# A fused decoder layer on one core: turning the gate's head pairs one at a time in buffers of their own, and issuing one kind of write from ScalarE

## The chip, the cores and the metric

The kernel runs on one core of one Trainium2 chip. The metric is device time of one execution in microseconds (us), the median of several runs. A kernel has five instruction streams: TensorE (PE, matrix products and 128x128 transposes), VectorE (DVE), ScalarE (ACT), GpSimd (POOL) and SyncE (SP). Each stream runs in order: an instruction that waits holds everything behind it on its own engine. DMA transfers are issued by SP, POOL or ACT, and run beside the engines.

## The reference

One decoder layer on 256 tokens of width 2048, all in float32: a normalised input goes through one wide projection, then through two token mixers, whose outputs are gated, projected, merged and added back.

```
h = rms_norm(x, pre_norm_w);  proj = h @ w_in
# A, gated delta rule, 8 heads x 128: conv + silu on q, k, v; chunks of 64 tokens
T = inverse(I + L);  u = T @ vb;  w = T @ kb;  scan over the chunks;  norm;  * silu(gdn_z)
# B, block attention, 8 heads x 128: at 256 tokens one block, so plain causal attention
p = softmax(mask(q @ k.T * scale));  ob = (p @ v) * silu(moba_z)
merged = sigmoid(gate_a) * (oa @ w_branch_a) + sigmoid(gate_b) * (ob @ w_branch_b)
out = x + rms_norm(merged @ w_out, post_norm_w)
```

The change concerns B: the factor `silu(moba_z)`, called `zm` here ("the gate"), and the probabilities `p`.

## The kernel before, in words

Every projection multiplies in three parts: a float32 weight block is cast by ScalarE into `hi` (line 256) and VectorE subtracts to get `lo` (line 257); PE then runs `hi` and `lo` products (line 167 is the helper that records every matmul). The weights arrive by DMA from SP into three rotating buffers, and the `hi`/`lo` pairs rotate over three more, so a cast can begin when PE has finished the block three before it. A block of a head projection is 16 matmuls. PE runs these projections back to back, block after block, in the order of the list `ORDER` (line 47): `zm0 zm1` are the gate's two projections, `mv0 mv1` attention's values, `v3` the last pair of values of mixer A, and `mk0 ... mk3` the query and key projections (`mq`, `mk`) of the four head pairs of mixer B.

Everything else is put between the projections by queues of generators. Each generator runs some instructions and yields a number, the wait until its next step, counted in half units per small group of matmuls (`tick`, line 159). Several queues advance beside each other; within one queue, one generator follows the other. `pin` (line 164) keeps an instruction in program order with the other pinned ones of its engine; what isn't pinned may be moved by the program's scheduler.

Four pieces of work of this kind meet around the change:

- **Inverse** (`inverse`, line 705): VectorE works out T in 63 steps on the tile `tv` (lines 726 and 733). Then POOL writes it to DRAM (`t_d`, line 737) and loads it back in another layout (`inv`, line 750). PE transposes it (`tl`) soon after.
- **Values of A** (`v_tok`, line 786): VectorE transposes in 32x32 blocks, and `moved` (line 779) finishes the transposition by a write to DRAM (line 783) and a load back (line 784): here `vx`.
- **Gate** (`turned_gate`, line 1250): the gate has tokens on the partitions and must have channels there. For each head pair VectorE makes two block transposes (line 1257) into the scratch `spare`, which is the last quarter of the tile `ga_`, and `moved` brings them back over `zm`. One generator does all four pairs, one after the other, in the queue `bq`; it starts with `mk0`. The scratch is one for all four pairs, and the same one that the probabilities use.
- **Attention** (`attend`, line 1190): scores `ms` on PE, softmax on VectorE and ScalarE, block transposes of the probabilities into `spare` (line 1222), `moved` with the write `pT_d` and the load `pT`, and after a wait of 5 the products `po` (lines 1232 and 1233), which read `pT`. VectorE multiplies them with the turned gate (line 1234).

In `moved`, both the write and the load are issued by POOL and pinned, so POOL's order is the order of the program: whoever comes later waits until the earlier transfers may be issued. The load must wait on POOL until the write has landed.

Of the kernel before, what the change touches and what calls it, by code (L numbers as in the profile page):

```python
# [15 lines left out]
P = 128  # L16
# [23 lines left out]
A_WAIT2 = 1.5  # L40
A_WAIT3 = 5
A_WAIT4 = 1
G_WAIT = 1.5

# [48 lines left out]
def hybrid_layer(  # L95
# [15 lines left out]
    nc = tc.nc  # L111
    B, S, D = x.shape
    NT = S // P
    KT = D // P
    H = a_log.shape[1]
# [31 lines left out]
    def aux_tile(name):  # L147
        return aux.tile([P, 512], F32, tag="aux", name=name)

    gq, vq, mq = Queue(), Queue(), Queue()  # L150
    aq, bq = Queue(), Queue()
# [3 lines left out]
    extra = []  # L155
# [8 lines left out]
    pin = tc.keep_in_program_order  # L164

    def mm(*args, **kwargs):
        return pin(nc.tensor.matmul(*args, **kwargs))  # L167
# [496 lines left out]
    zg, zm = z_tiles["zg"], z_tiles["zm"]  # L664
# [14 lines left out]
    def silu_gate(n, c):  # L679
        c0, c1 = (ZG[c], ZG[c + 1]) if n == "zg" else (c * 512, (c + 1) * 512)  # L680
        silu_out(n, c0, c1, proj_n(w_in, {"zg": CZ, "zm": CMZ}[n] + c0, hT, KT, f"{n}{c}", c1 - c0))
# [3 lines left out]
    def keys(p):  # L685
        pk = proj_t(CK + 2 * p * P, f"k{2 * p}")
        kTs[p] += [halves(pk[m], f"k{2 * p + m}") for m in range(2)]
        for m in range(2):
            conv_silu(kTs[p][m], H + 2 * p + m)

    def queries(p):
        h = 2 * p
        pq = proj_t(CQ + h * P, f"q{h}")
        qTs = [halves(pq[m], f"q{h + m}") for m in range(2)]
        for m in range(2):
            conv_silu(qTs[m], h + m)
        gq.add(score_pair(h, kTs[p], qTs))
        if p == H // 2 - 1:
            gq.add(inverse())
            gq.add(solve())  # L700
# [75 lines left out]
            nc.vector.tensor_scalar_mul(inv[t][lo_, :, 64:128], pb[t][lo_], -1.0)  # L776
        yield SV_WAIT

    def moved(blocks, back, name):

        n = blocks.shape[1] // 4
        d = dram.tile([4, P, n], F32, name=f"{name}_d")
        pin(nc.gpsimd.dma_start(d.rearrange("i (r j) x -> (i r) (j x)", j=4), blocks))
        pin(nc.gpsimd.dma_start(back.rearrange("p (i x) -> p i x", i=4), d.rearrange("i k x -> k i x")))

    def v_tok(h, vTs):
# [23 lines left out]
    def values(p):  # L810
        h = 2 * p
        pv_ = proj_t(CV + h * P, f"v{h}")
        vTs = [halves(pv_[m], f"v{h + m}") for m in range(2)]
        for m in range(2):
            conv_silu(vTs[m], 2 * H + h + m)
        vq.add(v_tok(h, vTs))
        v_left[0] -= 1
        after[0] = SLOW

    ga_ = big.tile([P, D // 512, NT, 512], F32, tag="ga", name="ga")  # L820

    spare = ga_[:, D // 512 - 1].rearrange("p t n -> p (t n)")
# [19 lines left out]
    def sigmoid_gate(n, col, c):  # L842
        pts = proj_n(w_in, col + c * 512, hT, KT, f"{n}{c}")
        for t in range(NT):
            nc.scalar.activation(gate_place(n, c, t), pts[t], AF.Sigmoid, scale=rstd[:, t : t + 1])
# [336 lines left out]
    def attention_values(c):  # L1182
        pts = proj_n(w_in, CMV + c * 512, hT, KT, f"mv{c}")
        for t in range(NT):
            nc.scalar.activation(mv[:, t, c * 512 : (c + 1) * 512], pts[t], AF.Copy, scale=rstd[:, t : t + 1])
# [4 lines left out]
    def attend(h, qTs, kTs):  # L1190
        yield A_WAIT1
        ss, mxs, sms = [], [], []
        for m in range(2):
            qT, kT = qTs[m], kTs[m]
            ps = aux_tile(f"ms_{h + m}")
            mm(ps[:, 0:P], qT[:, :P], kT[:, :P], start=True, stop=True)
            mm(ps[:, P : 3 * P], qT[:, P:], kT, start=True, stop=True)
            s = wk.tile([P, 3 * P], F32, tag="s", name=f"s_{h + m}")
            mx = wk.tile([P, 2], F32, tag="mx", name=f"mx_{h + m}")
            sm = wk.tile([P, 2], F32, tag="sm", name=f"sm_{h + m}")  # L1200
            nc.vector.scalar_tensor_tensor(
                s[:, 0:P], ps[:, 0:P], qscale[:, 0:1], mask_m[:, P:], op0=ALU.mult, op1=ALU.add
            )
            nc.vector.scalar_tensor_tensor(
                s[:, P:], ps[:, P : 3 * P], qscale[:, 1:2], mask_m, op0=ALU.mult, op1=ALU.add
            )
            nc.vector.tensor_reduce(mx[:, 0:1], s[:, 0:P], axis=AX.X, op=ALU.max, negate=True)
            nc.vector.tensor_reduce(mx[:, 1:2], s[:, P:], axis=AX.X, op=ALU.max, negate=True)
            nc.scalar.activation(s[:, 0:P], s[:, 0:P], AF.Exp, bias=mx[:, 0:1], accum_out=sm[:, 0:1])
            nc.scalar.activation(s[:, P:], s[:, P:], AF.Exp, bias=mx[:, 1:2], accum_out=sm[:, 1:2])  # L1210
            nc.vector.reciprocal(sm, sm)
            ss.append(s)
            sms.append(sm)
        yield A_WAIT2
        for s, sm in zip(ss, sms):
            nc.scalar.activation(s[:, 0:P], s[:, 0:P], AF.Copy, scale=sm[:, 0:1])
            nc.scalar.activation(s[:, P:], s[:, P:], AF.Copy, scale=sm[:, 1:2])
        yield 0.5
        blocks = spare[:, : 6 * P]
        to = blocks.rearrange("p (i m b r) -> p m b i r", i=4, m=2, b=3)  # L1220
        for m in range(2):
            nc.vector.transpose(to[:, m], ss[m].rearrange("p (b c i) -> p b i c", b=3, i=4))
        back = wk.tile([P, 6 * P], F32, tag="pT", bufs=1, name=f"pT_{h}")
        moved(blocks, back, f"pT_{h}")
        pT = back.rearrange("p (j m b r) -> p m b j r", j=4, m=2, b=3)
        attended[0] += 2
        yield A_WAIT3
        gate = zm()[:, h // 2].rearrange("p t x -> p (t x)").rearrange("p (j m t r) -> p m t j r", j=4, m=2, t=NT)
        for m in range(2):
            po = aux_tile(f"po_{h + m}")  # L1230
            hc = slice((h + m) * P, (h + m + 1) * P)
            mm(po[:, :S], mv[:, 0, hc], pT[:, m, 0:2], start=True, stop=False)
            mm(po[:, P:S], mv[:, 1, hc], pT[:, m, 2], start=False, stop=True)
            nc.vector.tensor_tensor(
                gate[:, m], po[:, :S].rearrange("p (t j r) -> p t j r", t=NT, j=4), gate[:, m], op=ALU.mult
            )
        bq.add(split_attention(h, gate))

    def split_attention(h, om):
        yield A_WAIT4  # L1240
        while not obs:
            yield 0.5
        obT = obs[0]
        for m in range(2):
            hi, lo = (obT[:, h + m, c0 : c0 + S].rearrange("p (t j r) -> p t j r", t=NT, j=4) for c0 in (0, S))
            nc.scalar.copy(hi, om[:, m])
            nc.vector.tensor_tensor(lo, om[:, m], hi.bitcast(F32), op=ALU.subtract)
        yield 0.5

    def turned_gate():  # L1250
        blocks = spare[:, : 4 * P]
        to = blocks.rearrange("p (i m t r) -> p t m i r", i=4, m=2, t=NT)
        for p in range(H // 2):
            yield G_WAIT
            x = zm()[:, p]
            for t in range(NT):
                nc.vector.transpose(to[:, t], x[:, t].rearrange("p (m c i) -> p m i c", m=2, i=4))
            moved(blocks, x.rearrange("p t x -> p (t x)"), f"zm_{p}")

    def attention(p):  # L1260
        h = 2 * p
        pq = proj_t(CMQ + h * P, f"mq{h}")
        qTs = [halves(pq[m], f"mq{h + m}") for m in range(2)]
        pk = proj_t(CMK + h * P, f"mk{h}")
        kTs = [halves(pk[m], f"mk{h + m}") for m in range(2)]
        for m in range(2):
            nc.vector.tensor_tensor(kTs[m], kTs[m], rrow, op=ALU.mult)
        aq.add(attend(h, qTs, kTs))
# [26 lines left out]
    for blk in ORDER:  # L1295
        n, c = blk[:2].rstrip("0123456789"), int(blk[-1])
        if n in ("q", "kq"):
            if n == "kq":
                keys(c)
            queries(c)  # L1300
        elif n in ("zg", "zm"):
            silu_gate(n, c)
        elif n == "v":
            values(c)
        elif n == "mv":
            attention_values(c)
        elif n == "mk":
            if not c:
                bq.add(turned_gate())
            attention(c)  # L1310
        elif n == "ua":
            branch_pair(c)
        else:
            sigmoid_gate(n, {"ga": CGA, "gb": CGB}[n], c)
# [248 lines left out]
```

## Time and profile before

| | |
|---|---|
| median of 3 runs | 766.59 us (766.3 to 767.48) |
| the profiled execution's own time | 765.81 us |
| its span, first to last instruction | 764.1 us |
| mean granted clock of TensorE | 0.994 of full speed |
| busy PE / DVE / ACT / POOL | 748.8 / 597.2 / 456.0 / 67.5 us |
| instructions | 10413 |

PE is busy for 98% of the span, so the profile is read from PE's idle time: where it stands still, for what, and at what clock it runs afterwards. A line of the timeline gives the start, the length, the engine, the source line, the operation with its tiles and their number, and in brackets the idle time of the engine before it and what ended it. The chain of waits follows the work that ended last backwards.

### The profile page before, as it was taken

To read this page: it belongs to the slowest core of one execution; us is meant where nothing else is said; L and a number is where in the kernel's file an instruction comes from. 1 tells how busy PE (TensorE), PEld (TensorE's weight loads), DVE (VectorE), ACT (ScalarE), POOL (GpSimd) and SP (SyncE) were. 2 spreads that over 40 slices of the span, in tenths; PEclk is the share of its full clock that TensorE was granted. 3 is DMA by queue.
4 is the path that set the end of the run, shared out by engine and by line. 5 is a ranking of instruction groups with operands and counts; after the bars stand their busy time and mean duration, and the time that the engine had idled before them with its cause. 6 is when DMAs were issued, how large, how long until landed. Compare 5 with 4: busy or idle time off the path is not lost.

```text
span 764.1 us, 10413 instructions
## 1 busy us (share of the span) xinstructions
PE 748.8 (98%) x3858; PEld 637.9 (83%) x3858; DVE 597.2 (78%) x963; ACT 456.0 (60%) x693; POOL 67.5 (9%) x101
## 2 busy tenths in 40 slices
PE   9999999999999999998899999999999999999996
PEld 7898988899888888877799888887888888888885
DVE  6878778986978999766358885778797778789864
ACT  6776666657655664545366475656556654765751
POOL 1000201112000000032001100101000101000000
PEclk9999999999999999999999999999999999999998
DMA  9585675467767566679247966798989777987962
GB/s 305 183 267 188 192 215 173 138 182 209 240 208 243 192 201 194 210 238 291 65 152 275 265 210 214 253 325 249 327 232 318 212 276 216 338 261 214 272 252 110
DMA packets 102424, 173.88 MB, mean 228 GB/s; under 512 B 3941, under 2 KB 49702, under 8 KB 101862
## 3 DMA queue, kind: packets, MB, share of 16 engines
q1 hardware_dynamic: 89094, 134.83, 54.0%
q0 software_dynamic: 12816, 37.76, 17.6%
q8 instruction: 30, 0.49, 0.2%
q10 hardware_dynamic: 464, 0.63, 0.2%
q14 instruction: 20, 0.16, 0.1%
HBM read 166.39 MB, written 6.82 MB: 227 GB/s over the span
## 4 chain that ended last, share of the span: by engine, by line
PE 91%; DMA 5%; DVE 2%; POOL 1%; issue 1%; ACT 0%; DVEq 0%; POOLq 0%
PE a_gb L167 12%; PE a_ga L167 11%; PE a_y L167 9%; PE a_ub L167 7%; PE a_k L167 6%; PE a_zg L167 6%; PE a_q L167 6%; PE a_v L167 6%; PE a_mv L167 6%; PE a_zm L167 6%; PE a_ua L167 4%; PE a_mk L167 3%; PE a_mq L167 3%; DMA zm_d<-ga 2%; PE s L167 1%; DMA pT_d<-ga 1%
## 5 line engine op out<-in xcount | busy, mean ns | idle before, releaser
L167 PE MATMUL a_gb<-hi_gb,hT 128*128 128x512 f32 x256 | 81.1, 391 | 0.0
L167 PE MATMUL a_ga<-hi_ga,hT 128*128 128x512 f32 x256 | 80.9, 391 | 0.0
L167 PEld LDWEIGHTS a_gb<-hi_gb,hT 128*128 128x128 f32 x256 | 48.0, 188 | 10.5
L167 PEld LDWEIGHTS a_ga<-hi_ga,hT 128*128 128x128 f32 x256 | 48.1, 188 | 10.2
L257 DVE TENSOR_TENSOR lo_ga<-raw_ga,hi_ga 128x1024 fp32r<-128x1024 f32 x32 | 39.0, 1221 | 15.3 <-ACT hi_ga L256 15.1
L256 ACT CAST hi_ga<-raw_ga 128x1024 fp32r<-128x1024 f32 x32 | 33.6, 1053 | 28.5 <-PE a_ga L167 19.3
L167 PE MATMUL a_gb<-lo_gb,hT 128*128 128x512 f32 x128 | 50.2, 392 | 0.1
L167 PE MATMUL a_ga<-lo_ga,hT 128*128 128x512 f32 x128 | 49.9, 390 | 0.0
L256 ACT CAST hi_gb<-raw_gb 128x1024 fp32r<-128x1024 f32 x32 | 33.5, 1051 | 25.6 <-PE a_gb L167 13.9
L257 DVE TENSOR_TENSOR lo_gb<-raw_gb,hi_gb 128x1024 fp32r<-128x1024 f32 x32 | 39.1, 1221 | 10.9 <-ACT hi_gb L256 10.6
L167 PE MATMUL a_zg<-hi_zg,hT 128*128 128x348 f32 (+1 forms) x192 | 46.7, 322 | 0.0
L167 PE MATMUL a_mq<-hT,hi_mq 128*128 128x512 f32 x128 | 42.2, 411 | 0.0
L167 PE MATMUL a_mk<-hT,hi_mk 128*128 128x512 f32 x128 | 40.4, 397 | 0.0
L167 PE MATMUL a_q<-hT,hi_q 128*128 128x512 f32 x128 | 40.2, 396 | 0.0
L167 PE MATMUL a_v<-hT,hi_v 128*128 128x512 f32 x128 | 40.2, 395 | 0.0
L167 PE MATMUL a_mv<-hi_mv,hT 128*128 128x512 f32 x128 | 40.0, 391 | 0.0
L167 PE MATMUL a_zm<-hi_zm,hT 128*128 128x512 f32 x128 | 39.6, 389 | 0.0
L167 PE MATMUL a_k<-hT,hi_k 128*128 128x512 f32 (+1 forms) x129 | 38.2, 397 | 0.1
L256 ACT CAST hi_mq<-raw_mq 128x1024 fp32r<-128x1024 f32 x16 | 16.8, 1049 | 31.9 <-PE a_mk L167 12.7
L167 PEld LDWEIGHTS a_zg<-hi_zg,hT 128*128 128x128 f32 x192 | 33.5, 188 | 0.1
L167 PE MATMUL a_zg<-lo_zg,hT 128*128 128x348 f32 (+1 forms) x96 | 30.9, 322 | 0.0
L167 PEld LDWEIGHTS a_mq<-hT,lo_mq 128*128 128x128 f32 x128 | 24.4, 191 | 6.9 <-DVE lo_mq L257 1.1
(468 smaller groups left out, 2026.7 us busy)
## 6 DMA issues: line engine op xcount, KB each, us to landing
raw_ga<-in_w_in_dram SPq DMA_DIRECT2D x16, 1024.0 KB, 5.2
raw_gb<-in_w_in_dram SPq DMA_DIRECT2D x16, 1024.0 KB, 6.0
raw_y<-in_w_out_dram SPq DMA_DIRECT2D x14, 1024.0 KB, 7.7
raw_q<-in_w_in_dram SPq DMA_DIRECT2D x8, 1024.0 KB, 5.5
raw_mv<-in_w_in_dram SPq DMA_DIRECT2D x8, 1024.0 KB, 5.0
raw_v<-in_w_in_dram SPq DMA_DIRECT2D x8, 1024.0 KB, 5.6
raw_zm<-in_w_in_dram SPq DMA_DIRECT2D x8, 1024.0 KB, 5.0
raw_mq<-in_w_in_dram SPq DMA_DIRECT2D x8, 1024.0 KB, 5.7
```

The costliest lines, as they stand in the source:

```text
L167: return pin(nc.tensor.matmul(*args, **kwargs))
L256: nc.scalar.copy(hi, raw)
L257: nc.vector.tensor_tensor(lo, raw, hi.bitcast(F32), op=ALU.subtract)
```

## The change

The gate's turning becomes one generator per pair, added with that pair's own query and key projections to a queue of its own (`zq`) instead of one generator for all. The wait before it is 4 for the first pair and 5 for the others. Its block transposes go into the third quarter of `ga_`, half of it for even and half for odd pairs, instead of the probabilities' scratch. Its transposes and those of the probabilities are pinned. And the write `pT_d` of the probabilities is issued by ScalarE instead of POOL; the load stays on POOL.

```
-G_WAIT = 1.5
+G_WAIT = (4, 5)
...
-    def moved(blocks, back, name):
+    def moved(blocks, back, name, writer=nc.gpsimd):
...
-        pin(nc.gpsimd.dma_start(d.rearrange("i (r j) x -> (i r) (j x)", j=4), blocks))
+        pin(writer.dma_start(d.rearrange("i (r j) x -> (i r) (j x)", j=4), blocks))
...
-            nc.vector.transpose(to[:, m], ss[m].rearrange("p (b c i) -> p b i c", b=3, i=4))
+            pin(nc.vector.transpose(to[:, m], ss[m].rearrange("p (b c i) -> p b i c", b=3, i=4)))
...
-        moved(blocks, back, f"pT_{h}")
+        moved(blocks, back, f"pT_{h}", nc.scalar)
...
-    def turned_gate():
-        blocks = spare[:, : 4 * P]
+    zq = Queue()
+    extra.append(zq)
+
+    def turned_gate(p):
+        yield G_WAIT[p > 0]
+        blocks = ga_[:, 2, p % 2]
         to = blocks.rearrange("p (i m t r) -> p t m i r", i=4, m=2, t=NT)
-        for p in range(H // 2):
-            yield G_WAIT
-            x = zm()[:, p]
-            for t in range(NT):
-                nc.vector.transpose(to[:, t], x[:, t].rearrange("p (m c i) -> p m i c", m=2, i=4))
-            moved(blocks, x.rearrange("p t x -> p (t x)"), f"zm_{p}")
+        x = zm()[:, p]
+        for t in range(NT):
+            pin(nc.vector.transpose(to[:, t], x[:, t].rearrange("p (m c i) -> p m i c", m=2, i=4)))
+        moved(blocks, x.rearrange("p t x -> p (t x)"), f"zm_{p}")
...
-            if not c:
-                bq.add(turned_gate())
+            zq.add(turned_gate(c))
             attention(c)
```

PE's instructions and SP's loads keep their order. Three places on other engines change.

**POOL, from the last pair of values to the first pair of probabilities.** In the names, `zm_1_d` is the gate's write of pair 1 (the pairs count from 0), `pT_0` the probabilities of heads 0 and 1, `pT_2` those of heads 2 and 3. Before:

```order
L783 DMA vx_6_d_3206<-vx_6_3203 128x512
L784 DMA vx_6_3203<-vx_6_d_3206 128x4x128
L783 DMA zm_1_d_3211<-ga_477 128x512
L784 DMA zm_2662<-zm_1_d_3211 128x4x128
L783 DMA zm_2_d_3260<-ga_477 128x512
L784 DMA zm_2662<-zm_2_d_3260 128x4x128
L783 DMA zm_3_d_3293<-ga_477 128x512
...
L784 DMA zm_2662<-zm_3_d_3293 128x4x128
L737 DMA t_d_476<-tv_1013 512x1x64 x4
L750 DMA inv_0_3428<-t_d_476 64x8x64 x2
L750 DMA inv_1_3432<-t_d_476 64x8x64 x2
L783 DMA pT_0_d_3477<-ga_477 128x768
```

And now, behind the same two rows of `vx`:

```order
L783 DMA zm_0_d_3226<-ga_477 128x512
L784 DMA zm_2662<-zm_0_d_3226 128x4x128
L737 DMA t_d_476<-tv_1013 512x1x64 x4
...
L750 DMA inv_0_3413<-t_d_476 64x8x64 x2
L750 DMA inv_1_3417<-t_d_476 64x8x64 x2
L784 DMA pT_0_3461<-pT_0_d_3462 128x4x192
L783 DMA zm_1_d_3505<-ga_477 128x512
L784 DMA zm_2662<-zm_1_d_3505 128x4x128
L784 DMA pT_2_3790<-pT_2_d_3791 128x4x192
L783 DMA zm_2_d_3838<-ga_477 128x512
```

Ahead of `t_d` stands one pair of the gate, pair 0, where there were three; the others follow the loads of the probabilities one by one, and the writes `pT_d` are gone from POOL.

**DVE, in the stage of the last head pair.** `lo_mk_0_1` is the low part of the second block of that pair's key projection, `a_mq` a query projection's bank. Before:

```order
L1222 STREAM_TRANSPOSE ga<-s_4081 128x3x4x32
L1222 STREAM_TRANSPOSE ga<-s_4094 128x3x4x32
L532 TENSOR_TENSOR y_mq_4140<-a_mq_0_3982,y_mq_4140 128x256
L532 TENSOR_TENSOR y_mq_4143<-a_mq_1_3983,y_mq_4143 128x256
L257 TENSOR_TENSOR lo_mk_0_1_4177<-raw_mk_0_4148,hi_mk_0_1_4176 128x1024
```

And now:

```order
L1222 STREAM_TRANSPOSE ga<-s_4076 128x3x4x32
L1222 STREAM_TRANSPOSE ga<-s_4089 128x3x4x32
L532 TENSOR_TENSOR y_mq_4135<-a_mq_0_3977,y_mq_4135 128x256
L532 TENSOR_TENSOR y_mq_4138<-a_mq_1_3978,y_mq_4138 128x256
L1259 STREAM_TRANSPOSE ga<-zm 128x2x4x32 x2
L257 TENSOR_TENSOR lo_mk_0_1_4177<-raw_mk_0_4143,hi_mk_0_1_4176 128x1024
```

The gate's two transposes of pair 3 now stand between the softmax and the low part of that block.

**ACT, in the stage of the second head pair.** `sv` are the solve's products on PE for mixer A, `gdn` their place in SBUF. Now:

```order
L256 CAST hi_mk_1_0_3883<-raw_mk_1_3881 128x1024
L531 COPY y_mq_3797<-a_mq_1_3600 128x256
L783 DMA pT_d<-ga 128x768
L1071 COPY gdn_468<-sv_0_0_3824 128x512
L256 CAST hi_mk_1_1_3919<-raw_mk_1_3881 128x1024
L1071 COPY gdn_469<-sv_0_1_3830 128x512
```

Before, the row of `pT_d` was not there, and the cast of `hi_mk_1_1` stood ahead of both copies. On DVE, the two transposes that `pT_d` waits for now come behind the two subtractions of line 1073, which wait for PE's `sv`.

## The prediction

> **What bounds the kernel now.** I read the page's busy times first, then the timeline of PE for its idle time, then the table by stretches for the clock, and last the chain of waits back from the longest wait.
>
> ```profile
> PE 748.8 (98%) x3858; PEld 637.9 (83%) x3858; DVE 597.2 (78%) x963; ACT 456.0 (60%) x693; POOL 67.5 (9%) x101
> ```
>
> PE stands still for 764.1 - 748.8 = 15.3 us. The change leaves PE's order as it was, so it can only win from that time and from PE's clock, or add to them. These are PE's waits inside the run:
>
> ```profile
> 330.43 0.50 PE L167 MATMUL a_mk<-hT,lo_mk 128*128 128x256 f32 x2 [0.76 <-DVE lo_mk L257]
> ...
> 336.91 0.50 PE L167 MATMUL a_mq<-hT,lo_mq 128*128 128x256 f32 x2 [0.64 <-DVE lo_mq L257]
> ...
> 339.18 0.92 PE L167 MATMUL ms<-y_mk,y_mq 128*128 128x128 f32 x4 [0.41 <-DVE y_mk L1267]
> ...
> 365.28 2.22 PE L167 MATMUL po<-pT,mv 128*128 128x256 f32 x8 [4.44 <-DMA pT<-pT_d]
> ```
>
> They make 0.76 + 0.64 + 0.41 + 4.44 = 6.25 us. By stretches (length, busy PE, PEld, DVE, ACT, POOL, granted clock, DMA share, GB/s):
>
> ```profile
> 330.00:340.00 10.00, 8.52 (x47) 6.92 (x48) 8.57 (x17) 3.98 (x6) 3.44 (x7) 1.00 0.82 248
> ...
> 360.00:370.00 10.00, 5.56 (x25) 4.52 (x24) 2.69 (x5) 1.31 (x4) 0.17 (x1) 0.83 0.36 125
> ...
> 700.00:764.10 64.10, 56.50 (x270) 47.16 (x268) 42.86 (x54) 31.36 (x47) 1.32 (x1) 0.96 0.68 217
> ```
>
> The end holds 7.6 us of the idle time and the start the remaining 1.4; neither is touched. The three short waits left the clock at 1.00. Behind the long one it was 0.83, and the chain of waits shows what that cost, beside the same work at full clock:
>
> ```profile
> 365.28 2.22 PE po L167 x8
> 367.50 2.35 PE a_mq L167 x8
> ...
> 382.94 2.79 PE a_mq L167 x16
> ...
> 408.59 1.31 PE po L167 x8
> ```
>
> 2.22 - 1.31 = 0.91 for `po`, and 2.35 - 2.79/2 = 0.95 for eight matmuls: 1.86 us. All that can be won here is 6.25 + 1.86 = 8.11 us. The chain that led to the wait (start, length, what):
>
> ```profile
> 324.21 3.87 DMA zm_d<-ga
> ...
> 334.28 4.46 DMA zm_d<-ga
> ...
> 339.02 0.75 POOL zm L784
> 339.77 1.86 POOL t_d L737 x3
> 341.63 6.32 DMA t_d<-tv
> ...
> 348.49 2.72 POOL inv L750 x4
> 351.20 7.91 DMA pT_d<-ga
> ...
> 359.39 5.84 DMA pT<-pT_d
> ```
>
> Three rounds of the gate, two of them shown, stand in POOL's queue from 324.21 to 339.77. Behind them wait `t_d`, then `inv`, then `pT_d`, then `pT`. VectorE is caught too, since the next round's transposes wait for the scratch:
>
> ```profile
> 328.10 1.17 DVE L1257 STREAM_TRANSPOSE ga<-zm 128x256 f32<-128x256 f32 x2 [4.40 <-DMA zm_d<-ga]
> ...
> 344.02 1.64 DVE L1222 STREAM_TRANSPOSE ga<-s 128x384 f32<-128x384 f32 x2 [0.53 <-ACT s L1217]
> ```
>
> The three short waits of PE follow from those 4.40 us. The probabilities were transposed by 345.66, but their write was issued at 351.20: 5.5 us behind POOL's queue.
>
> **The gate, one pair at a time.** In POOL's queue one round stays ahead of `t_d`, pair 0's. Its write starts at 324.2 as the first round did (the `vx` load ahead of it is unchanged to some tenths), lands 3.87 later, and with 0.3 of issue and 0.75 for the load `t_d` may start at 329.2. `tv` must be ready as well:
>
> ```profile
> 326.23 1.05 ACT L256 CAST hi_mq<-raw_mq 128x1024 fp32r<-128x1024 f32 x1 [1.74 <-PE a_mk L167]
> ...
> 333.91 0.15 DVE L726 TENSOR_TENSOR tw<-lc,tv 128x32 f32<-128x32 f32 x1
> ...
> 334.54 0.19 DVE L733 TENSOR_TENSOR tv<-tv,tw 128x16 f32<-128x16 f32 x1
> ```
>
> Its last four steps (first and last shown) take 334.73 - 333.91 = 0.8 and now stand behind the subtraction that follows this cast (327.3 + 1.2 = 328.5): 329.3. So `t_d` starts 10.4 us earlier, its last part lands at 329.3 + 1.86 + 6.32 = 337.5, and POOL is through with `inv` by 338.0 + 2.72 = 340.7, before any probabilities are ready. VectorE's 4.40 us are gone, so PE's three short waits go: 1.81 us, and everything paced by PE comes 1.81 earlier.
>
> **The probabilities' write on ScalarE.** Ahead of it there stand a copy that needs PE's next bank, and one cast. The copy is like the first row here, and the bank is complete where the block of the second row starts:
>
> ```profile
> 333.78 0.37 ACT L531 COPY y_mk<-a_mk 128x256 f32<-128x256 f32 x1
> ...
> 344.13 0.62 PE L167 MATMUL a_mq<-hT,hi_mq 128*128 128x512 f32 x2
> ```
>
> 344.13 - 1.81 = 342.3; copy and cast (0.37 + 1.05) bring the issue to 343.8. The transposes end at 345.66 - 1.81 = 343.85 or sooner, so I take 343.9. How long a write on this queue takes isn't shown; the same write from POOL, and an issue on ScalarE's queue, bound it:
>
> ```profile
> DMA to landing us min/median/max: 2.6/4.7/7.9
> ...
> 0.81 0.41 ACTq L193 DMA_DIRECT2D rawf_k<-in_w_in_dram  x1
> ```
>
> It lands at 346.5 at the earliest and 351.8 at the latest; with 0.3 of issue and the load's 5.84, `pT` is there between 352.6 and 357.9. I take the late end, which is the one measured at this place (the row at 351.20). PE asked for `pT` at 365.28 - 4.44 = 360.84 and now asks at 359.0. The wait is gone with 1.1 us to spare, and the low clock with it. Had the write stayed on POOL, that queue would have been free at 340.7, so I give ScalarE's part of the change 0 us: the 5.5 us behind POOL's queue go with the gate already.
>
> The Trainium skill, "DMA: Bandwidth & Descriptors", section "Issuing engines are not separate DMA queues", says that transfers from any issuing engine share the same 16 DMA engines and interleave, and that a second issuer saves issue time only. By it the write on ScalarE wouldn't land sooner for being there: the late end, and the same sum. No row here shows it yet.
>
> **What is added.** The eight gate transposes and four writes stay, in other places; ScalarE gets four issues of some 0.4 us, in 40% idle time. A low part must end before PE's first `lo` matmul of its block, and four places come close.
>
> ```profile
> 316.77 1.21 DVE L257 TENSOR_TENSOR lo_mk<-raw_mk,hi_mk 128x1024 fp32r<-128x1024 f32 x1
> 317.90 0.63 DVE L792 STREAM_TRANSPOSE vx<-y_v 128x256 f32<-128x256 f32 x1
> ...
> 321.15 0.40 PE L167 MATMUL a_mk<-hT,lo_mk 128*128 128x256 f32 x2
> ...
> 346.92 0.63 PE L167 MATMUL a_mk<-hT,hi_mk 128*128 128x512 f32 x2
> ...
> 418.63 1.62 DVE L1222 STREAM_TRANSPOSE ga<-s 128x384 f32<-128x384 f32 x2 [0.53 <-ACT s L1217]
> ...
> 420.97 2.36 DVE L257 TENSOR_TENSOR lo_mk<-raw_mk,hi_mk 128x1024 fp32r<-128x1024 f32 x2
> ...
> 422.67 0.39 PE L167 MATMUL a_mk<-hT,lo_mk 128*128 128x256 f32 x2
> ```
>
> Pair 0's transposes and one of `vx` (1.17 + 0.6) come ahead of a low part that ended at 318.0: 319.7 against 321.15. Pair 1's come while PE's key projection (from 346.92 - 1.81 = 345.1) is fed: its first low part ends at 343.8 + 1.2 = 345.0 against 345.1 + 0.47, its second, behind the copy of the next bank at 345.1, a cast and a subtraction, at 347.8 against 348.4. Pair 2's stand inside the softmax, and the low parts behind them still wait for their casts. Pair 3's don't fit: the `lo_mk` that starts at 420.97 gets 1.17 ahead of it and starts at about 422.0 (the transposes overlap what precedes by a tenth or so); it ends at 423.2, and PE wants it at 422.67. I add 0.5 us for PE (0 if VectorE gains a little more on the way, 1.2 if all of it counts).
>
> **Sum**, against the profiled execution: 764.1 - 6.25 - 1.86 + 0.5 = 756.5 span, and 765.81 - 764.1 = 1.7 around it: 758.2. That execution lies 0.78 below the median of 766.59, so the median forecast is 766.59 - 7.6 = **759.0 us**.
>
> **Rivals.** (1) The probabilities are late again, by less. For it speaks the spare 1.1 us, made of a write whose landing has varied by 5.3; against it that I took the late end already. PE then waits between 0 and the old 4.44; half of it, 2.2, gives 761.2, and a wait of 4 gives 763.0.
>
> (2) The low clock of 360 to 370 isn't from the wait and stays, or comes back elsewhere: 759.0 + 1.86 = 760.9. Against it: 0.83 stands only in the stretch with the long wait. The Trainium skill, "TensorE: Matmul & The Clock Gate", section "Part 1: The HAM clock gate", halves the clock after an idle window of about 3.4 us until as long a busy one has passed; by it the loss would be an estimated 1.7 us and the three short waits free, and the trace agrees (1.86; 1.00).
>
> (3) A load that was hidden shows. The cast below waited for its weights, and the copies of the inverse behind it feed `ltl`, which PE reached only after the long wait:
>
> ```profile
> 358.69 1.05 ACT L256 CAST hi_mq<-raw_mq 128x1024 fp32r<-128x1024 f32 x1 [2.11 <-DMA raw_mq<-in_w_in_dram]
> 359.64 1.06 ACT L764 COPY tmp<-tl 64x512 f32<-64x512 f32 x2
> ```
>
> PE now wants `ltl` at 359.0 + 1.31 + 1.40 = 361.7; even if the weights come no sooner the copies end at 360.7. Weights 3 us later still would cost 2.0: 761.0.
>
> (4) Slower: ScalarE, in order, is held by `pT_d` of the second pair, whose transposes now stand behind the subtractions of line 1073.
>
> ```profile
> 387.75 1.28 DVE L1073 TENSOR_TENSOR gdn<-gdn,sv 128x512 f32<-128x512 f32 x2
> ...
> 396.66 5.57 PE a_mk L167 x32
> ```
>
> In the times of the profile the transposes end at 389.0 + 1.64 = 390.7. Behind ScalarE's wait stands the cast for the second half of those 32 matmuls, which needs its low part near 399.9: the cast must start by 399.9 - 1.05 - 1.22 = 397.6, 6.9 us later. Only a hold past 397.6 + 7.6 = 405.2 makes the kernel slower; one to 406 gives 766.59 + 0.8 = 767.4.
>
> (5) The change doesn't do what it says: POOL's queue holds `t_d` or `pT` as long as before, and the time stays at 766.6.
>
> **How the numbers follow.** The forecast gets 0.74, rival (1) 0.10, (2) 0.05, (3) 0.05, (4) 0.03, (5) 0.03. Less than 0.2% (1.5 us) is what a measurement of this kernel can hardly tell from no change. The first four cases are faster by more than that: 0.94; (5) is the same, 0.03; (4) slower, 0.03. The low end is no new stall (758.5) less 1.1 for the runs' spread (766.3 to 767.48): 757.4. The high end takes in (2), (3) and rival (1) up to a wait of 4: 763.0.
>
> **What would show it.** Right: the chain of waits stays on PE from 310 to 440; no wait of PE for `pT`; the clock 1.00 in every stretch from 320 to 420; `t_d` issued near 329, `pT_d` near 344, `pT` landed by 358; one short wait of PE for `lo_mk` some 8 us ahead of 422.7; PE busy near 747. Wrong: a wait at `po` or `ltl`; a low clock anywhere in the middle; a cast held behind `pT_d` on ScalarE; `t_d` behind 331, which would mean that `vx` or the first round of the gate, not the queue, sets it.

## The result, and the profile after

The changed kernel takes 757.77 us, median of 4 runs (757.3 to 758.54); the kernel before, beside it, 767.04 us (4 runs, 766.3 to 768.6). The ratio is 0.9878 with a 95% interval of [0.9859, 0.9897]: 9.3 us, or 1.2%, faster. The forecast was 759.0 us, 757.4 to 763.0. The profiled execution took 757.3 us with a span of 755.6 us, 8.5 us less than the 764.1 us before.

From the page of the changed kernel, its busy times and the shares of its chain of waits:

```profile
PE 746.3 (99%) x3858; PEld 636.6 (84%) x3858; DVE 597.6 (79%) x963; ACT 456.0 (60%) x693; POOL 65.3 (9%) x97
...
PE 96%; DVE 2%; ACT 1%; DMA 0%; issue 0%; DVEq 0%; ACTq 0%
```

From its view of waits, all of PE's added up (total, times, longest):

```profile
PE warm L167 <- DVE ones L183: 1.1, 1, 1.1
PE a_mk L167 <- DVE lo_mk L257: 0.3, 1, 0.3
PE pnc L170 <- DMA nrow<-in_pre_norm_w_dram: 0.2, 1, 0.2
```

The chain of waits that ended last is PE's own work for 96% of the span. Between 310 and 440 us it leaves PE once, from 403.56 to 414.22, by way of VectorE's and ScalarE's work on the probabilities to `lo_mk`. Between the start and the end of the program one wait of PE is left, 0.3 us for `lo_mk`. The four waits of before are gone. PE's busy time fell by 2.5 us although it does the same work, mostly because the low clock had stretched its matmuls (1.71 us of it, worked out below). The table by stretches, in the columns of the prediction's, shows the two stretches that had held most of the loss:

```profile
330.00:340.00 10.00, 10.00 (x59) 8.78 (x58) 7.77 (x17) 5.97 (x15) 4.34 (x7) 1.00 0.96 280
...
360.00:370.00 10.00, 10.00 (x100) 8.98 (x99) 4.41 (x8) 3.26 (x4) 0.00 (x0) 1.00 0.38 109
```

From 360 to 370 PE was busy for 5.56 us at a clock of 0.83; now it is busy throughout at 1.00. POOL's queue in its order of time (start, length, idle time before):

```profile
324.42 0.55 POOL L783 DMA_DIRECT2D zm_d<-ga  x1
330.54 0.76 POOL L784 DMA_DIRECT2D zm<-zm_d  x1 [5.57 <-ACT y_mk L531]
331.29 2.60 POOL L737 DMA_DIRECT2D t_d<-tv  x4
...
340.01 2.74 POOL L750 DMA_DIRECT2D inv<-t_d  x4 [5.09 <-DMA t_d<-tv]
346.15 0.78 POOL L784 DMA_DIRECT2D pT<-pT_d  x1 [3.41 <-DMA pT_d<-ga]
```

One round of the gate stands ahead of `t_d` instead of three. `t_d` starts at 331.29 (339.77 before) and the load of `pT` at 346.15 (359.39 before). The DMA view gives that load 4.0 us to landing, so `pT` is there by about 350.2, and PE comes to `po` at 358.24. The probabilities' write, on VectorE, ScalarE and ScalarE's queue:

```profile
340.75 1.62 DVE L1222 STREAM_TRANSPOSE ga<-s 128x384 f32<-128x384 f32 x2 [0.53 <-ACT s L1217]
...
341.99 1.05 ACT L256 CAST hi_mk<-raw_mk 128x1024 fp32r<-128x1024 f32 x1
342.40 0.35 ACTq L783 DMA_DIRECT2D pT_d<-ga  x1
```

The write is issued at 342.40, while the cast ahead of it still runs (341.99 to 343.04).

### The profile page after: what moved, and what is told of

It reads as the page before. It is cut to its first block, busy times and chain, and to the rows that moved or that the text cites. A ratio compares the mean times of both kernels' runs of the same rounds, so it can differ in the third digit from the quotient of the medians.

```text
span 755.6 us, 10416 instructions
## 1 busy us (share of the span) xinstructions
PE 746.3 (99%) x3858; PEld 636.6 (84%) x3858; DVE 597.6 (79%) x963; ACT 456.0 (60%) x693; POOL 65.3 (9%) x97
## 4 chain that ended last, share of the span: by engine, by line
PE 96%; DVE 2%; ACT 1%; DMA 0%; issue 0%; DVEq 0%; ACTq 0%
PE a_gb L167 12%; PE a_ga L167 11%; PE a_y L167 9%; PE a_ub L167 7%; PE a_zg L167 6%; PE a_k L167 6%; PE a_q L167 6%; PE a_v L167 6%; PE a_mv L167 6%; PE a_zm L167 6%; PE a_mk L167 6%; PE a_mq L167 5%; PE a_ua L167 4%; PE s L167 1%; PE so L167 1%; PE sv L167 1%
## 5 line engine op out<-in xcount | busy, mean ns | idle before, releaser
L256 ACT CAST hi_zg<-raw_zg 128x696 fp32r<-128x696 f32 (+1 forms) x24 | 18.5, 772 | 19.1 <-PE a_zg L167 9.0
```

The source lines that it names most:

```text
L256: nc.scalar.copy(hi, raw)
```

## The experiments

My theory was that all of the gain is PE's waits: the three short ones go with VectorE's stall, the long one and its low clock go because POOL's queue is free in time. Each experiment takes one piece of that apart. Ratios are to the kernel before, measured beside each.

| experiment | median us | ratio, 95% interval |
|---|---|---|
| gate alone | 758.04 | 0.9886 [0.9871, 0.9900] |
| writes on ScalarE alone | 761.55 | 0.9930 [0.9911, 0.9950] |
| gate's buffers alone | 765.02 | 0.9967 [0.9955, 0.9980] |
| changed kernel, one scratch | 758.13 | 0.9890 [0.9874, 0.9905] |
| last pair's gate later | 757.69 | 0.9882 [0.9866, 0.9898] |
| `po` later, queues as before | 763.62 | 0.9953 [0.9933, 0.9974] |
| last pair's gate thrice | 758.5 | one execution |
| last pair's gate five times | 760.64 | one execution |
| `pT` held, 23 memsets | 764.28 | 0.9966 [0.9953, 0.9979] |
| `pT` held, 28 memsets | 766.10 | 0.9995 [0.9983, 1.0007] |

### The gate alone

```diff
-        moved(blocks, back, f"pT_{h}", nc.scalar)
+        moved(blocks, back, f"pT_{h}")
```

> The changed kernel with the probabilities' writes (pT_d) back on POOL; the gate stays as changed. My theory: POOL is free of the inverse's loads at 342.75 us in the changed kernel's trace (340.01 + 2.74) and the transposes end at 342.37, so the write leaves POOL about 0.4 us later than ScalarE issued it, pT lands well before PE asks for it at 358.24, and the time stays at 757.8 +- 0.8 us: ScalarE's part is worth 0. The rival: the write's place on ScalarE carries part of the gain, because the queue of POOL is what was 5.5 us late; then PE's wait for pT comes back and the time is 760 to 766.

It takes 758.04 us, the same as the changed kernel's 757.77. POOL's rows:

```profile
340.38 2.74 POOL L750 DMA_DIRECT2D inv<-t_d  x4 [5.41 <-DMA t_d<-tv]
343.10 0.58 POOL L783 DMA_DIRECT2D pT_d<-ga  x1
347.18 0.77 POOL L784 DMA_DIRECT2D pT<-pT_d  x1 [3.49 <-DMA pT_d<-ga]
```

POOL issues the write 0.7 us later than ScalarE did, and the load of `pT` leaves 1.03 us later. It takes 6.7 us to landing here, so `pT` is there by 353.9, and PE comes to `po` at 358.20: 4.3 us to spare. Behind the gate's change ScalarE's part is worth nothing that these runs can show. The Trainium skill, "DMA: Bandwidth & Descriptors", section "Issuing engines are not separate DMA queues", says that transfers from all issuing engines run on the same 16 DMA engines, and that a second issuer saves issue time only. The runs agree: from issue to the load behind it 3.75 us on ScalarE's queue (342.40 to 346.15) and 4.08 us on POOL's (343.10 to 347.18, 0.58 of it POOL's own issue).

### The writes on ScalarE alone

The kernel before with the second part of the change only:

```diff
-    def moved(blocks, back, name):
+    def moved(blocks, back, name, writer=nc.gpsimd):
...
-        pin(nc.gpsimd.dma_start(d.rearrange("i (r j) x -> (i r) (j x)", j=4), blocks))
+        pin(writer.dma_start(d.rearrange("i (r j) x -> (i r) (j x)", j=4), blocks))
...
-        moved(blocks, back, f"pT_{h}")
+        moved(blocks, back, f"pT_{h}", nc.scalar)
```

> The kernel before with only the second part of the change: ScalarE issues the probabilities' writes, the gate is turned as before. My theory: the write leaves at about 345.7 us (end of the transposes) instead of 351.20 and has landed by 350 to 353; POOL issues the load when its inverse's loads are through, at 351.2 to 353.5, instead of 359.39; pT is there at 357 to 359.4, ahead of the 360.84 at which PE asks. Then PE's long wait and the low clock behind it go (about 6.4 us), the three short waits (0.76, 0.64, 0.41 us shown) stay: 766.6 - 6.4 = about 760.2 us. So ScalarE's part, worth 0 behind the gate's change, would be worth most of the gain alone. The rival, that only the gate's rounds on POOL matter: 766.6, with the wait for pT still near 4.4.

It takes 761.55 us: more than half of the gain, from a part that adds nothing to the other. PE's waits between start and end, ScalarE's issue, and POOL:

```profile
332.40 0.51 PE L167 MATMUL a_mk<-hT,lo_mk 128*128 128x256 f32 x2 [2.24 <-DVE lo_mk L257]
338.99 0.50 PE L167 MATMUL a_mq<-hT,lo_mq 128*128 128x256 f32 x2 [0.74 <-DVE lo_mq L257]
341.25 0.92 PE L167 MATMUL ms<-y_mk,y_mq 128*128 128x128 f32 x4 [0.40 <-DVE y_mk L1267]
...
347.76 0.35 ACTq L783 DMA_DIRECT2D pT_d<-ga  x1
...
330.35 0.75 POOL L784 DMA_DIRECT2D zm<-zm_d  x1 [5.29 <-DMA zm_d<-ga]
...
350.84 2.75 POOL L750 DMA_DIRECT2D inv<-t_d  x4 [6.33 <-DMA t_d<-tv]
353.56 0.79 POOL L784 DMA_DIRECT2D pT<-pT_d  x1
```

The write no longer waits for `inv`, so the load of `pT` follows `inv` at once, and the long wait is gone although three rounds of the gate still stand ahead of `t_d`. The short waits stay as expected. One is longer than before, 2.24 us instead of 0.76, because the gate's first write took longer to land (5.29 us of idle time ahead of its load, where the same row of the kernel before has 3.61); that is about what the time lies over the expected 760.2. The rival, nothing gained, falls.

### The gate's buffers alone

The kernel before with four scratch buffers for the pairs, in the same place of the program:

```diff
     def turned_gate():
-        blocks = spare[:, : 4 * P]
-        to = blocks.rearrange("p (i m t r) -> p t m i r", i=4, m=2, t=NT)
         for p in range(H // 2):
             yield G_WAIT
+            blocks = ga_[:, 1 + p // 2, p % 2]
+            to = blocks.rearrange("p (i m t r) -> p t m i r", i=4, m=2, t=NT)
             x = zm()[:, p]
```

> The kernel before with four scratch buffers for the gate's pairs (no pair waits for another's write, none for the probabilities'), the gate's rounds in the same order on POOL as before, all writes on POOL. My theory: VectorE's 4.40 us idle and PE's three short waits go, and PE comes to po about 2.6 us sooner; but POOL still has three rounds (about 5 us each) ahead of t_d, so pT lands within 1 us of where it did (365.3 us) and PE's wait for it grows from 4.44 to 6 or 7 us. Time 765 to 767: nothing is won by the buffers alone. The rival, that VectorE's stall is the cause of all the waits: about 758 to 761.

765.02 us, 2.3 us less than the kernel before: a small gain, where I had expected none. The gate's transposes in the groups of VectorE, of the kernel before (first row) and of this one (second), the last column their idle time and what ended it:

```profile
L1257 DVE STREAM_TRANSPOSE ga<-zm 128x256 f32<-128x256 f32 x8 | 4.8, 629 | 5.7 <-DMA zm_d<-ga 5.7
```

```profile
L1257 DVE STREAM_TRANSPOSE ga<-zm 128x256 f32<-128x256 f32 x8 | 4.8, 628 | 0.0
```

VectorE's stall is gone, and with it all three short waits. PE's only wait in the middle, and the rows of POOL that set it:

```profile
363.78 2.93 PE L167 MATMUL po<-pT,mv 128*128 128x256 f32 x8 [4.43 <-DMA pT<-pT_d]
...
341.11 0.76 POOL L784 DMA_DIRECT2D zm<-zm_d  x1 [2.29 <-DMA zm_d<-ga]
341.86 2.61 POOL L737 DMA_DIRECT2D t_d<-tv  x4
```

The wait for `pT` stays at 4.43 us. So VectorE's stall and POOL's queue are two causes: the buffers cure the first and leave the second. I had expected the wait to grow to 6 or 7 us; `pT` came 1.5 us sooner than before, as PE did (359.35 against 360.84), and part of what the three waits gave was paid back in clock: by stretches of a quarter of a microsecond PE works at half clock from 363.78 to 368.79, which loses 2.5 us, where the kernel before lost 1.71.

### The changed kernel with one scratch

All pairs in the one scratch that the probabilities use too; ScalarE still issues the probabilities' writes:

```diff
-        blocks = ga_[:, 2, p % 2]
+        blocks = spare[:, : 4 * P]
```

> The changed kernel with the gate's pairs turned with their own projections as changed, but all in the one scratch that the probabilities use too (no buffers of their own); ScalarE issues the probabilities' writes. My theory: with the pairs 90 us apart a write has landed long before the scratch is wanted again, except where the gate's transposes stand closely behind the probabilities' (pair 1 near 344 us and pair 3 near 412 us): VectorE is held there for up to the landing of pT_d, 3.4 us, of which 0 to 1.5 us reaches PE. 757.8 to 759.5 us: the spacing carries the gain, not the buffers. The rival: without the buffers VectorE's stall of 4.4 us returns, and with it PE's short waits and a late pT: 761 to 766.

758.13 us, as the changed kernel. Its gate's transposes:

```profile
L1259 DVE STREAM_TRANSPOSE ga<-zm 128x256 f32<-128x256 f32 x8 | 4.6, 613 | 0.0
```

They never wait: turned each with its own projections, a pair finds the scratch free. The places carry the gain, and the buffers that came with them none that can be measured. A kernel with neither the buffers nor ScalarE's writes was not run, and the pinning of the transposes, which all these kernels have, was not taken out by itself.

### The last pair's gate later

```diff
-G_WAIT = (4, 5)
+G_WAIT = (4, 5, 5, 8)
...
-        yield G_WAIT[p > 0]
+        yield G_WAIT[p]
```

> The changed kernel with only the last pair's gate transposes (L1259) moved behind the low parts of its key projection. My theory: the last short wait of PE, 0.3 us for lo_mk at 414 us, goes, and with it 0.6 us of start-to-start time: 757.2 us, 0.08% less than the changed kernel, which five rounds can't tell from it; the trace decides: PE's only waits are those of the start, and the stretch from po of pair 1 (399.67) to the first a_ga (422.40) shrinks from 22.73 to about 22.1 us. The rival: the wait only moves to another low part (lo_ga or y_mk) and the stretch stays at 22.7.

757.69 us, 0.08 us under the changed kernel, which no timing here can tell apart. The chain of waits of the changed kernel and of this one, from pair 1's `po` to the first `a_ga`:

```profile
399.67 1.31 PE po L167 x8
...
413.06 1.12 DVE lo_mk L257
414.22 8.19 PE a_mk L167 x46
422.40 4.11 PE a_ga L167 x18
```

```profile
400.63 1.31 PE po L167 x8
...
411.61 11.15 PE a_mk L167 x64
422.76 4.19 PE a_ga L167 x18
```

22.73 us became 22.13 us, and no wait is left in this stretch: taking away an idle time of 0.31 us took 0.60 us from the path.

### The transposes of the last pair repeated

The same four transposes' work done three times in one kernel, five times in another:

```diff
-            pin(nc.vector.transpose(to[:, t], x[:, t].rearrange("p (m c i) -> p m i c", m=2, i=4)))
+            for _ in range(2 + 1 if p == 3 else 1):
+                pin(nc.vector.transpose(to[:, t], x[:, t].rearrange("p (m c i) -> p m i c", m=2, i=4)))
```

> The changed kernel with the last pair's gate transposes done three times (four transposes more, 0.58 us each, 2.3 us of VectorE ahead of lo_mk; the same values are written again). My theory: PE's wait for lo_mk near 414 us grows from 0.3 to about 2.6 us and the time by 2.3 us to about 760.1; the clock stays at 1.00 behind it, so a wait of this size costs its idle time plus some 0.3 us and no more. The rival, that every wait is followed by a low clock that the stretches of 10 us don't resolve: 761.5 or more, and a clock below 1.00 in 410 to 430.

> The changed kernel with the last pair's gate transposes done five times (eight transposes more, 4.7 us of VectorE ahead of lo_mk; the same values are written again). My theory: PE's wait for lo_mk grows from 0.3 to about 5.0 us, as long as the wait for pT in the kernel before (4.44), and the clock behind it falls as it did there (0.83 over 10 us), which costs about 1.9 us more: 757.8 + 4.7 + 1.9 = 764.4 us. The rival, that the low clock of the kernel before was no consequence of the wait: clock 1.00 and 762.5 us.

Both expectations missed. The repeats didn't stay in one block: the builder set low parts between them, and VectorE had slack there. In the first kernel (758.5 us) PE's wait for `lo_mk` is 0.26 us, no longer than the 0.31 us of the changed kernel; in the second (760.64 us) the added time became two waits:

```profile
420.65 0.51 PE L167 MATMUL a_mk<-hT,lo_mk 128*128 128x256 f32 x2 [0.78 <-DVE lo_mk L257]
425.14 0.50 PE L167 MATMUL a_ga<-lo_ga,hT 128*128 128x512 f32 x1 [1.67 <-DVE lo_ga L257]
```

The clock was 1.00 in all stretches around them. So 2.3 us more of VectorE's time cost nothing that one execution can show, and these waits left the clock alone, as the one of 2.24 us did in the kernel with the writes alone. What a long wait does had to be tried elsewhere.

### `po` later in PE's order

The kernel before, queues and buffers untouched:

```diff
-        yield A_WAIT3
+        yield A_WAIT3 + (2 if h == 0 else 0)
```

> The kernel before with the first pair's po two steps later in PE's order (the wait count behind its transposes raised by 2; later pairs' work moves along with it), all queues and buffers as before. My theory: PE comes to po at about 368 us by the times of the profile of before, after pT has landed at 365.3, so the 4.44 us wait and the 1.86 us of low clock behind it go although POOL's queue is as late as before; the three short waits stay: about 760.2 us, up to 763 where the later softmax of the next pair costs something new. The clock is 1.00 in every stretch from 330 to 400. The rival of the prediction, that the low clock isn't from the wait: it stays near 0.83 in the stretch from 360 to 370 and the time is 762 or more.

763.62 us, over the expected 760.2 to 763. The wait for `pT` went, as expected, and the clock is 1.00 from 360 to 370. But the low clock appeared in another place, behind a wait for `lo_mk` that this time was 2.57 us long:

```profile
333.57 0.74 PE L167 MATMUL a_mk<-hT,lo_mk 128*128 128x256 f32 x2 [2.57 <-DVE lo_mk L257]
```

The stretch right behind that wait has the clock at 0.50:

```profile
334.00:337.00 3.00, 3.00 (x11) 2.61 (x11) 1.67 (x3) 0.00 (x0) 0.58 (x1) 0.50 0.86 237
```

That speaks for the low clock as a consequence of a wait, wherever the wait stands. The wait for `lo_mk`, the low clock and two small waits (0.8 and 0.3 us) account for all but about 1 us of the time over the changed kernel's; that rest is open.

### `pT` held back

The changed kernel with memsets on POOL ahead of the first load of `pT`, 23 in one kernel, 28 in the other:

```diff
+        if name == "pT_0":
+            for _ in range(23):
+                pin(nc.gpsimd.memset(back[:, :512], 0.0))
         pin(nc.gpsimd.dma_start(back.rearrange("p (i x) -> p i x", i=4), d.rearrange("i k x -> k i x")))
```

> The changed kernel with 23 memsets of pT (128x512, about 0.5 us each by the row of the inverse's memsets) on POOL ahead of the first pair's load of pT, which overwrites them: POOL is free at 342.75, the load leaves near 354.3 instead of 346.15, and with the 5.84 us that it took in the kernel before pT lands near 360.1, while PE asks at 358.24. This is the prediction's rival (1) made on purpose. My theory: PE waits about 2 us at po, the clock stays at 1.00 (the wait of 2.24 us in the run of the writes alone left it so), and the time is the changed kernel's 757.8 + 2 + 0.3 (what a wait costs beyond the idle time that the profile shows) = about 760.1 us, 758 to 762 by what a memset really takes. The rival, that any wait at po brings the low clock: 761.8 and 0.83 in 360 to 370.

> The same with 28 memsets: pT lands some 2.5 us later than with 23, and PE waits about 4.5 us at po, as in the kernel before. My theory: the clock falls behind the wait to half for 3 to 5 us, which costs 1.7 to 2.4 us, and the time is 757.8 + 4.5 + 0.3 + 2 = about 764.5 us; taken from the kernel before's 766.6 that leaves only the three short waits (2.6 us by start to start) less the changed kernel's own 0.6. So a late pT alone gives back 6 to 7 of the 9 us. The rival, that the low clock of the kernel before came from somewhere else: clock 1.00 and 762.6 us.

764.28 and 766.10 us. A memset took 0.58 us, not 0.5, so the waits are longer than planned. Of the kernel with 23 first PE's wait, then its stretches, where the clock is the third column from the right:

```profile
362.85 2.90 PE L167 MATMUL po<-pT,mv 128*128 128x256 f32 x8 [3.37 <-DMA pT<-pT_d]
```

```profile
360.00:362.00 2.00, 0.00 (x0) 0.00 (x0) 0.00 (x0) 0.00 (x0) 0.00 (x0) 1.00 1.07 392
362.00:366.00 4.00, 3.15 (x10) 2.72 (x11) 0.63 (x2) 0.00 (x0) 0.75 (x1) 0.51 0.32 115
366.00:369.00 3.00, 3.00 (x15) 2.49 (x14) 0.22 (x1) 1.04 (x1) 0.00 (x0) 0.51 0.02 8
```

The same of the kernel with 28:

```profile
365.35 2.90 PE L167 MATMUL po<-pT,mv 128*128 128x256 f32 x8 [5.90 <-DMA pT<-pT_d]
```

```profile
361.00:362.00 1.00, 0.00 (x0) 0.00 (x0) 0.00 (x0) 0.00 (x0) 1.00 (x2) 0.79 0.03 10
362.00:366.00 4.00, 0.65 (x2) 0.59 (x3) 0.00 (x0) 0.00 (x0) 0.28 (x1) 0.50 0.60 164
366.00:368.00 2.00, 2.00 (x9) 1.73 (x7) 0.42 (x1) 0.00 (x0) 0.75 (x1) 0.50 0.17 43
```

A late `pT` alone brings back the wait, the low clock and, with a wait of 5.90 us, the whole time of the kernel before. The shorter wait has the dearer clock. Behind 3.37 us PE works at half clock from 362.85 to 368.95, which loses 6.1 / 2 = 3.05 us. Behind 5.90 us it does so from 365.35 to 368.40, which loses 1.5 us: the rest of the low stretch lay inside the wait, where it costs nothing. From `po` on the two kernels lose 3.37 + 0.27 + 3.05 = 6.7 us and 5.90 + 0.27 + 1.5 = 7.7 us by these rows (the 0.27 is explained below). My expected 760.1 and 764.5 missed by the waits' lengths and, in the first, by the clock, which I had at 1.00 for a wait of 2 us; the rival stated for it (a low clock behind this wait) was the better one. Since this wait came out at 3.37 us, what a wait of 2 us does at `po` is not shown.

## Why the prediction was right, and where it was off

**The direction and the causes hold.** The four waits that the prediction added up are the ones that went, and the experiments confirm two separate causes: VectorE's stall (gone in the kernel with buffers alone, together with the three short waits) and POOL's queue (the wait for `pT` stays there, and comes back when the load is held).

**The mis-sized term is the price of PE's waits**, which the prediction took as their idle time: 6.25 us for four waits. Around the wait for `lo_mk`, in the kernel before and at the same matmuls of the changed kernel, PE's rows are:

```profile
329.04 0.63 PE L167 MATMUL a_mk<-hT,hi_mk 128*128 128x512 f32 x2
330.43 0.50 PE L167 MATMUL a_mk<-hT,lo_mk 128*128 128x256 f32 x2 [0.76 <-DVE lo_mk L257]
330.77 0.63 PE L167 MATMUL a_mk<-hT,hi_mk 128*128 128x512 f32 x2
```

```profile
329.06 0.63 PE L167 MATMUL a_mk<-hT,hi_mk 128*128 128x512 f32 x2
329.53 0.40 PE L167 MATMUL a_mk<-hT,lo_mk 128*128 128x256 f32 x2
329.76 0.63 PE L167 MATMUL a_mk<-hT,hi_mk 128*128 128x512 f32 x2
```

From one `hi` pair to the next it is 1.73 us with the wait and 0.70 us without: 1.03 us for an idle time of 0.76. In a full pipeline a pair starts 0.16 us before the end that the profile gives the pair ahead (0.47 against 0.63), and the first pair behind a wait takes 0.11 us longer to hand over (0.34 against 0.23). Together that is 0.27 us, and the same reckoning at the other two short waits gives 0.26 and 0.28. The experiment that removed the last wait found 0.60 us for 0.31, so 0.29.

**The sum with that price closes.** Idle time 6.25, four times 0.27 = 1.08, low clock 1.71 (3.41 us at 0.50, below), less the new wait of 0.31 + 0.27 = 0.58: 8.46 us. The spans differ by 8.5. The prediction had 8.11 and 0.5: 7.6. Its 1.86 for the low clock had part of the 0.27 in it, and the new stall came where it was put (414.22 for 422.7 - 8) with 0.31 us of idle time.

The medians differ by 9.3 us, 0.8 more than the spans. The kernel before varies by over 2 us from run to run, and two things could make that much. One is the low clock's length: 3.41 us in its profile, 6.83 us behind the same wait in the kernel with buffers alone. Over the 35 runs of the kernel before that were taken beside the experiments, the 14 with a mean clock of 0.992 average 767.6 us, the 14 with 0.996 average 766.4, which speaks for it. The other is the gate's first write, which landed after 3.9 us in the profile of before and after 5.6 us in the kernels with the writes alone and with `po` later; there PE's wait for `lo_mk` was 2.24 and 2.57 us instead of 0.76. No profile of a slower run of the kernel before shows which it was, so it stays open.

**Steps that were off without a price.** `t_d` was to start at 329.3 and started at 331.29. The last step of `tv` was ready in time, but the gate's first write took 5.6 us to land instead of the 3.87 taken from before (324.42 to about 330.0; its load left at 330.54, and the profile puts the last of that wait down to a copy of ScalarE). So the first round of the gate, not `tv`, sets `t_d`; the prediction had named a start behind 331 as the sign of that. Three other steps came out sooner and outweighed it. The issue of `pT_d` came at 342.40 instead of 343.9, since VectorE was 3.3 us ahead and not 1.8 (transposes ended at 342.37, before at 345.66), and since ScalarE's issue didn't wait for the end of the cast. The write had landed by 346.15, ahead of the earliest time of its range (346.5), not at the late end that was taken. And the load took 4.0 us instead of 5.84, which was luck: with the gate alone it took 6.7. So `pT` has about 8 us to spare where 1.1 were forecast, and rival (1) never came close.

**ScalarE's part at 0 us** was right for this change, and the reason (POOL is free by the time the probabilities are) held in the kernel with the gate alone. The prediction did not say that the part alone is worth more than half of the gain; two cures of one wait don't add up.

**The other rivals.** (2) The clock is 1.00 in every stretch from 320 to 420: the low clock was from the wait. The Trainium skill, "TensorE: Matmul & The Clock Gate", section "Part 1: The HAM clock gate", was cited for a low clock after about 3.4 us of idle time. The runs show it after less: behind 2.57 us, and in the kernel with 23 memsets some 2.6 us after the last matmul. The measurement decides. (3) PE does not wait at `ltl`. (4) ScalarE is held by the second pair's write, but at no cost: its work ends at 377.93, the write is issued at 381.68, and the copy behind it had to wait until 382.31 for PE's `sv` anyway. PE's next wait is the one at 414.22. (5) fell with the time.

## What to carry to other kernels

Price a wait of TensorE by the start-to-start time of the instructions around it, not by its idle time alone: here 0.27 us more for each, and 1.5 to 3 us lost to half clock behind each of the five waits of 2.57 us or more, none behind those of 2.24 us or less. Where two edits each cure the same late transfer, measure each alone before keeping both: here the kernel without the buffers (758.13 us) and the one without ScalarE's writes (758.04) are as fast as the one with both (757.77). A first-in queue that carries write-and-reload pairs delays everything behind it by whole round trips (`t_d` left at 339.77 behind three of them, at 331.29 behind one), so look at what stands ahead in the queue before looking at the transfer itself.

## What the runs showed of the hardware

The low clock came in two lengths. Stretches of a quarter of a microsecond put it at 3.41 us in the kernel before and in the one with `po` later, and at 6.83 us, twice that, in the kernel with buffers alone and in both with `pT` held; inside it the clock was 0.50. It began 0.8 us after the wait's end in the kernel before, whose rows are

```profile
365.00:366.00 1.00, 0.72 (x4) 0.67 (x5) 0.00 (x0) 0.00 (x0) 0.00 (x0) 1.00 0.00 0
366.00:369.00 3.00, 3.00 (x11) 2.54 (x11) 0.85 (x2) 0.00 (x0) 0.00 (x0) 0.51 0.00 0
```

and its two ends

```profile
366.00:366.25 0.25, 0.25 (x3) 0.25 (x3) 0.00 (x0) 0.00 (x0) 0.00 (x0) 0.59 0.00 0
...
369.25:369.50 0.25, 0.25 (x2) 0.15 (x2) 0.00 (x0) 0.00 (x0) 0.00 (x0) 0.59 0.00 0
```

A mean of 0.59 between 1.00 and 0.50 means that 0.82 of the quarter, 0.205 us, was low: from 366.045 to 369.455. In the kernel with `po` later it began 0.1 us after the wait's end, and where `pT` was held, and with buffers alone, inside the wait. This fits the account of the Trainium skill, "TensorE: Matmul & The Clock Gate", section "Part 1: The HAM clock gate", that activity is watched in windows of about 3.4 us that run freely and do not start anew with a kernel. A wait would then be dear or cheap by where it falls in them. If so, the runs give bounds for a window's share of idle time: 2.1 of 3.41 us brought the low clock (28 memsets, the window that ends at 361.57), 1.8 did not (the kernel before, the window that ends at 362.63, of which 360.84 to 362.63 was idle). The wait of 2.24 us that left the clock alone fits only if it lay across the edge of two windows, which no row shows. All this is read from a few executions, not tested by moving a wait of one length through the windows.

A DMA issue on ScalarE's queue took 0.35 us and ran beside a cast of the same engine (342.40, in a cast from 341.99 to 343.04), so it took no time from ScalarE's work there. It still stands in ScalarE's order: what is behind it waits until its data is ready, as at 381.68.
